# Moving the weight sums and a low part among the instructions of a feed-forward chunk, and four low parts of the head to adding transfers

## The chip, the cores and the metric

The kernel runs on one core of a Trainium2 chip. The metric is the device time of one execution in microseconds. A core has five engines that each work through their own instructions in order and wait for each other by semaphores: TensorE (PE in the profile; PEld is its loading of weights), VectorE (DVE), ScalarE (ACT), GpSimd (POOL) and SyncE (SP). SyncE starts the plain transfers here; GpSimd starts a few transfers that add what they bring to what stands at their destination.

## The reference

Two request groups of 512 and 256 tokens (768 in all, width 1024) go through two layers with shared weights: windowed attention in the first, a gated short convolution in the second. Each is followed by a feed-forward block of width 4096 and a gated input embedding. All is in float32. The change lies in the feed-forward block of both layers:

```python
h = rms_norm(x, norm_mlp[i])
x = x + jnp.square(jax.nn.relu(h @ mlp_w_up[i])) @ mlp_w_down[i]
gate = jax.nn.sigmoid(rms_norm(x, norm_ple[i]) @ ple_w_gate[i])
x = x + (p[i] @ ple_w_proj[i]) * gate
```

## The kernel before

**Precision.** TensorE multiplies a rounded format (float32r). To keep float32's accuracy each operand is split into a high part (ScalarE copies it, rounded) and a low part (VectorE subtracts the high part from the original). A product is then three matmuls: high by high, high by low, low by high. For a sum `s` the weights' parts are named `zhi`/`zlo` (s2 and s3), `whi`/`wlo` (the others) and `vhi`/`vlo` (w22).

**Seven products for eight.** Most blocks are multiplied by Strassen's scheme in Winograd's form: weights and activations are quartered, sums and differences of quarters are formed (weights: s1 to s4; activations: t1 to t4), and seven products replace eight. `product7` is one of them: 12 matmuls of 384 columns, in a fixed order of w11, s3, s2, w12, s1, w22, s4. The sums of weights are made by VectorE (`sums32`: L411 and L412; `sums14`: L416 and L417), their high part by ScalarE (L436), their low part by VectorE (L455). The four banks of results a, b, c, d are made by adding and by copying: `c` is a copy of a behind w11, `d` one behind s2, both by ScalarE, and `p` a copy of b to SBUF; the next product then writes on into a.

**Feed-forward.** It has 16 up chunks (u = 0 to 15, each makes 256 of the 4096 hidden features) and down chunks of the same size; after u=0 and u=1 follow, seven times, an up chunk with even u, two down chunks, and an up chunk with odd u. So from u=3 on two up chunks stand together, odd and even, and two down chunks behind them. Each job prepares the weights of the next (`v`, made by `make`), while its own come as `w`. Up chunks are `up_begun`/`up_first` (u=0), `up_plain` (u=1, without the seven products) and `up` (from u=2 on, where `first` is true for u=2 alone).

**What sets the order.** The order of instructions of TensorE, VectorE and ScalarE is the one in which the code is written (`manual_schedule`). In `up`, `late()` takes the next of eight steps that turn the activations of the chunk before into parts: the last square, two high parts, the sums, two more high parts (L356), and the two low parts of the sums (`low`, L362, VectorE). Between the products stand: the weights' sums and parts for the next chunk; the addition of a and p behind s1 (L1279), which must be done before product s4 writes on into a; the rectifications (L1031, VectorE), and the squares (L1034, ScalarE). The low part of s32 of the weights is made at the start of the next job by `w.low("s32")`, where `due` says that it is still missing. The next job's first copy (`c` at L1256, or the two `C` at L1307 of a down chunk) stands on ScalarE behind the two squares.

**The head.** `up_first` is the chunk u=0 of layer 0. Beside its plain products it makes the sums of activations of the input for m = 1, 2 and 3 (`Sums`: `t13`, `t42` on VectorE, `high` on ScalarE, `low` on VectorE), from two copies `q` (L327). Their parts are first read by the product s3 of u=2. `Weights7.added` (L442) already makes a low part without VectorE: ScalarE writes the negative of the high part, and a transfer by GpSimd adds the original from outside of the chip.

Of the kernel before, what the change touches and what calls it, by code (L numbers as in the profile page):

```python
# [11 lines left out]
F32 = mybir.dt.float32  # L12
F32R = mybir.dt.float32r
AF = mybir.ActivationFunctionType
ALU = mybir.AluOpType
# [32 lines left out]
def trunk_kernel(ctx: ExitStack, tc: tile.TileContext, a: dict, out: bass.AP):  # L48
    nc = tc.nc
    act, dve, pe = nc.scalar, nc.vector, nc.tensor  # L50
# [54 lines left out]
    def bank(tag, name):  # L105
        return psum.tile([P, 512], F32, tag=tag, name=name, bufs=BANKS[tag])
# [45 lines left out]
    def big(name, dt=F32):  # L152

        nonlocal turn
        if more is None:
            return tmp.tile([P, T], dt, tag="t", name=name)
        turn += 1
        return tmp.tile([P, T], dt, tag=f"q{turn % 6}", name=name, bufs=1)
# [174 lines left out]
    class Sums:  # L333
# [26 lines left out]
        def low(self, i):  # L360
            hi, lo = self.t[i]
            dve.tensor_tensor(lo[:], (self.q1, self.q2)[i][:], hi[:].bitcast(F32), ALU.subtract)  # L362

        def steps(self):
            return [
                self.t13,
                lambda: self.high(0),
                self.t42,
                lambda: self.high(1),
                lambda: self.low(0),  # L370
                lambda: self.low(1),
            ]
# [24 lines left out]
    class Weights7:  # L397
# [44 lines left out]
        def added(self, group):  # L442

            self.high(group)
            self.due.remove(group)
            hi, lo, _ = self.parts[group]
            act.activation(lo[:], hi[:].bitcast(F32), AF.Copy, scale=-1.0)
            nc.gpsimd.dma_start(lo[:], self.src[group == "second"], accum_op=ALU.add)
# [20 lines left out]
    def product7(ps, w, key, xs, start, step=P, col=0):  # L469

        hi, lo = w.w[key]
        rhs = xs[QS7[key]]
        ks = [(slice(step * i + col, step * i + col + P), rhs[i]) for i in range(512 // step)]
        terms = [(hi[:, c], p) for c, ps_ in ks for p in ps_] + [(lo[:, c], ps_[0]) for c, ps_ in ks]
        for i, (a, b) in enumerate(terms):
            pe.matmul(ps, lhsT=a, rhs=b, start=start and i == 0, stop=i == len(terms) - 1, skip_group_check=True)  # L476
# [544 lines left out]
    def mlp(l, norm, nxt, w, places, early, product=None, begun=None):  # L1021
# [8 lines left out]
        def rectified(t, src, o, e, op):  # L1030
            dve.scalar_tensor_tensor(t[:, o:e], src, 0.0, r[:, o:e], op, ALU.mult)  # L1031

        def squared(t):
            act.activation(t[:], t[:], AF.Square)  # L1034

        def acts_of(u, y1, y2, rest):

            own = places[7 * (u % 2) : 7 * (u % 2) + 7]
            e = Acts(y1, y2, own, groups[u // 2], u % 2)
            if u < 2 * NG - 2:  # L1040
                return [
                    lambda: squared(rest),
                    lambda: e.highx(0),
                    lambda: (e.highx(1), e.lowx(0), e.lowx(1), e.t13()),
                    e.t42,
                    lambda: e.high(0),
                    lambda: e.high(1),
                    lambda: e.low(0),
                    lambda: e.low(1),
                ]  # L1050

            def whole(i, q):
                hi, lo = slot(own[2 * i], "act"), slot(own[2 * i + 1], "act")
                split(hi[:], lo[:], q[:])
                groups[u // 2].setdefault("whole", {})[u % 2, i] = hi[:], lo[:]

            return [lambda: squared(rest), lambda: whole(1, y2), lambda: whole(0, y1)]

        def late(n=1):

            for _ in range(n):
                if pend:
                    pend.pop(0)()

        def plain_block(ps, i, w, ks=range(KB)):
            for k in ks:
                m, h = PAIRED[k] % (KB // 2), PAIRED[k] // (KB // 2)
                c = slice(P * m, P * m + P)
                hi, lo = w.w[f"w{i + 1}{h + 1}"]
                for j, (wt, part) in enumerate(((hi, 0), (hi, 1), (lo, 0))):  # L1070
                    for o in range(2):
                        pe.matmul(
                            ps[o],
                            lhsT=wt[:, c],
                            rhs=xs[f"x{h + 1}{1 + o}"][m][part],
                            start=k == 0 and j == 0,
                            stop=k == KB - 1 and j == 2,
                        )
# [28 lines left out]
        def up_first(ps, w, v, parts, s1):  # L1107


            nonlocal r  # L1110
            plain_block(ps[0], 0, w, range(4))
            ss = norm.sum_squares(psum, parts=parts, tag="C")
            plain_block(ps[0], 0, w, range(4, KB))
            plain_block(ps[1], 1, w)
            logs, newton, result = norm.rstd_steps(psum, ss)
            logs()
            s1.t13()
            s1.t42()
            s1.high(0)
            s1.high(1)  # L1120
            newton()
            s2 = norm.copied(2, 6)
            result()
            r = norm.r
            v.added("second")
            s1.low(0)
            s1.low(1)
            v.high("direct")
            s2.t13()
            s2.high(0)  # L1130
            v.low("direct")
            s2.t42()
            s2.high(1)
            s3 = norm.copied(3, 7)
            s2.low(0)
            s2.low(1)
            y = [big(f"y{i + 1}") for i in range(2)]
            for i in range(2):
                for o in range(2):
                    rectified(y[i], ps[i][o], H * o, H * o + H, ALU.max)  # L1140
                if i == 0:
                    s3.t13()
                    s3.high(0)
                    squared(y[0])
                    s3.t42()
                    s3.high(1)
                    s3.low(0)
                    s3.low(1)
            pend.extend(acts_of(0, *y, y[1]))
            return v  # L1150

# [89 lines left out]
        def up(u, w, make, then):  # L1241


            first = u == PLAIN[l]
            w.low("s32")
            w.split("s14")
            if not first:
                late()
            v = make()
            seven = isinstance(v, Weights7)  # L1250
            a = bank("A", "a")[:, :H]
            product7(a, w, "w11", xs, True)
            if not first:
                late()
            c = bank("A" if first else "C", "c")[:, :H]
            act.activation(c, a, AF.Copy)  # L1256
            late(5 if first else 1)
            w.split("w22")
            late()
            b = bank("A" if first else "B", "b")[:, :H]  # L1260
            product7(b, w, "s3", xs, True)
            p = big("p")[:, :H]
            act.activation(p, b, AF.Copy)
            if seven:
                v.sums32()
            product7(a, w, "s2", xs, False)
            d = bank("B", "d")[:, :H]
            act.activation(d, a, AF.Copy)
            late(2)
            if seven:  # L1270
                v.sums14()
                v.high("s32")
            late()
            product7(c, w, "w12", xs, False)
            if seven:
                v.high("direct")
            product7(a, w, "s1", xs, False)
            y1, y2 = big("y1"), big("y2")
            dve.tensor_tensor(y2[:, H:], a, p, ALU.add)  # L1279
            rectified(y1, c, 0, H, ALU.max)  # L1280
            late()
            if seven:
                v.low("direct")
            else:
                v = [then(0)]
            product7(d, w, "w22", xs, False)
            dve.tensor_tensor(y2[:, :H], d, p, ALU.add)
            rectified(y2, y2[:], 0, T, ALU.min)
            squared(y2)
            product7(a, w, "s4", xs, False)  # L1290
            rectified(y1, a, H, T, ALU.max)
            pend.extend(acts_of(u, y1, y2, y1))
            return v
# [80 lines left out]
        with tc.manual_schedule(engines={ET.Activation, ET.PE, ET.DVE}):  # L1374
            for i, (job, *args) in enumerate(jobs):

                def make():

                    if i + 1 == len(jobs):
                        return None  # L1380
                    what, *n = jobs[i + 1]
                    if what is not down:
                        return up_chunk(l, *n)
                    k = (KB // 2) * n[0] + 2 * n[1]
                    return Weights7(a_down[k], a_down[k + 1])
# [544 lines left out]
```

## Time and profile before

| | |
|---|---|
| median of three runs | 1682.73 us (1681.79 to 1683.66) |
| the profiled execution | 1684.2 us |
| span of its records | 1682.2 us |
| TensorE's granted clock over the span | 0.996 |
| instructions in the span | 24112 |

A row of the timeline gives the start and the duration in microseconds, the engine, the line, the operation, what it writes and reads, and how many instructions were merged into the row; in brackets, how long the engine had been idle before it and for whom it waited. TensorE's matmuls overlap, so a row's end is later than the next row's start. A row of the waits gives who waited for whom, then the total in microseconds, the number of times and the longest.

### The profile page before, as it was taken

Reading aid. Unit: us, or ns where it says so; the run is one execution under the profiler, and the core shown is the slowest. Engines: PE = TensorE matmul, PEld = TensorE weight load, DVE = VectorE, ACT = ScalarE, POOL = GpSimd, SP = SyncE. Lnnn points to the kernel's source line nnn. Section 1 sums busy time; section 2 is a strip of 40 time slices with the busy share of each in tenths; the row PEclk is TensorE's granted clock in tenths of the full one; section 3 lists DMA queues with packets and bytes.
Section 4 is the critical chain, followed back from the end, with each engine's and each line's share of the span. In section 5 each row is a group of like instructions: output and inputs, shape, how many; then the busy total and the mean of one; then the engine's idle time right before and its main releaser. Section 6 shows DMA issues by size and latency. Waiting matters only on the chain.

```text
span 1682.2 us, 24112 instructions
## 1 busy us (share of the span) xinstructions
PE 1645.5 (98%) x9410; PEld 1586.8 (94%) x9410; DVE 1411.9 (84%) x2302; ACT 905.8 (54%) x1451; POOL 20.3 (1%) x46
## 2 busy tenths in 40 slices
PE   8999999999999999999999999999999999999996
PEld 6888788999999999999999999999999999999985
DVE  6598888899999999977788787768999898998776
ACT  6377756755555455545654334545555545554544
POOL 0211000000000000000000000000000000000000
PEclk9999999999999999999999999999999999999998
DMA  8755322411221222231312222121222122122222
GB/s 262 192 152 143 92 66 74 121 63 63 76 76 64 75 76 66 73 104 63 101 60 76 76 75 76 61 66 54 73 75 76 63 76 76 63 76 88 82 76 95
DMA packets 47107, 145.64 MB, mean 87 GB/s; under 512 B 6112, under 2 KB 9184, under 8 KB 46992
## 3 DMA queue, kind: packets, MB, share of 16 engines
q1 hardware_dynamic: 45168, 139.89, 26.1%
q0 software_dynamic: 1824, 4.20, 1.2%
q8 instruction: 74, 1.21, 0.3%
q14 instruction: 41, 0.34, 0.1%
HBM read 124.14 MB, written 10.48 MB: 80 GB/s over the span
## 4 chain that ended last, share of the span: by engine, by line
PE 58%; DVE 30%; ACT 7%; issue 3%; DMA 1%; SPq 0%; DVEq 0%; ACTq 0%
PE a L476 17%; PE mm L129 9%; PE mm L138 8%; PE b L476 4%; PE B L476 4%; PE C L476 3%; DVE t L362 3%; DVE wlo L455 3%; DVE y L1031 3%; PE gate L138 3%; DVE zlo L455 2%; DVE act L395 1%; PE pt L743 1%; DVE sum L412 1%; ACT y L1034 1%
## 5 line engine op out<-in xcount | busy, mean ns | idle before, releaser
L436 ACT ACTIVATE whi<-sum 128x1024 fp32r<-128x1024 f32 x67 | 70.5, 1053 | 150.7 <-PE a L476 146.8
L1034 ACT ACTIVATE y<-y 128x768 f32<-128x768 f32 x64 | 53.7, 840 | 135.5 <-DVE y L1031 135.5
L476 PE MATMUL a<-xs,whi 128*128 128x384 f32 x624 | 121.9, 337 | 2.4 <-DVE y L1279 1.7
L476 PEld LDWEIGHTS a<-xs,whi 128*128 128x128 f32 x624 | 110.0, 188 | 3.1 <-DVE y L1279 2.0
L476 PE MATMUL a<-t,zhi 128*128 128x384 f32 x536 | 109.1, 337 | 0.0
L476 PE MATMUL a<-t,whi 128*128 128x384 f32 x536 | 108.8, 336 | 0.0
L476 PE MATMUL b<-t,zhi 128*128 128x384 f32 x536 | 108.8, 336 | 0.0
L476 PE MATMUL a<-act,whi 128*128 128x384 f32 x448 | 96.5, 337 | 0.0
L476 PEld LDWEIGHTS a<-t,whi 128*128 128x128 f32 x536 | 94.9, 188 | 0.0
L476 PEld LDWEIGHTS a<-t,zhi 128*128 128x128 f32 x536 | 94.6, 188 | 0.2 <-ACT c L1752 0.2
L476 PEld LDWEIGHTS b<-t,zhi 128*128 128x128 f32 x536 | 94.8, 188 | 0.0
L455 DVE TENSOR_TENSOR wlo<-wraw,whi 128x1024 fp32r<-128x1024 f32 x70 | 85.3, 1218 | 7.6 <-ACT whi L436 7.6
L455 DVE TENSOR_TENSOR wlo<-sum,whi 128x1024 fp32r<-128x1024 f32 x67 | 81.9, 1222 | 8.9 <-ACT whi L436 8.9
L1312 DVE TENSOR_TENSOR x<-x,a 128x384 f32<-128x384 f32 x112 | 60.7, 552 | 33.8 <-PE a L476 33.5
L436 ACT ACTIVATE zhi<-sum 128x1024 fp32r<-128x1024 f32 x67 | 71.0, 1060 | 23.0 <-DVE sum L412 23.0
L138 PE MATMUL mm<-xs_mix,whi 128*128 128x512 f32 (+1 forms) x320 | 83.0, 342 | 0.0
L455 DVE TENSOR_TENSOR zlo<-sum,zhi 128x1024 fp32r<-128x1024 f32 x67 | 81.5, 1217 | 0.0
L476 PEld LDWEIGHTS a<-act,whi 128*128 128x128 f32 x448 | 79.8, 188 | 0.0
L436 ACT ACTIVATE whi<-wraw 128x1024 fp32r<-128x1024 f32 x72 | 75.7, 1051 | 6.2 <-PE C L476 6.2
L356 ACT ACTIVATE t<-y 128x768 fp32r<-128x768 f32 x56 | 47.1, 842 | 40.6 <-DVE y L347 29.9
L476 PE MATMUL a<-xs,wlo 128*128 128x384 f32 x312 | 67.1, 336 | 0.0
L455 DVE TENSOR_TENSOR vlo<-wraw,vhi 128x512 fp32r<-128x512 f32 x67 | 46.1, 689 | 24.8 <-ACT vhi L436 24.8
(338 smaller groups left out, 4503.7 us busy)
## 6 DMA issues: line engine op xcount, KB each, us to landing
wraw<-in_up SPq DMA_DIRECT2D x64, 512.0 KB, 3.5
wraw<-in_down SPq DMA_DIRECT2D x64, 512.0 KB, 3.5
wraw<-in_w_in SPq DMA_DIRECT2D x24, 512.0 KB, 3.5
wraw<-in_gate SPq DMA_DIRECT2D x16, 512.0 KB, 3.4
pj<-pjs SPq DMA_DIRECT2D x16, 384.0 KB, 3.8
wraw<-in_w_q SPq DMA_DIRECT2D x8, 512.0 KB, 4.5
wraw<-in_w_out SPq DMA_DIRECT2D x8, 512.0 KB, 3.4
x_in<-in_x SPq DMA_DIRECT2D x8, 384.0 KB, 7.3
```

The source lines that it names most:

```text
L129: pe.matmul(t, lhsT=w, rhs=x[:, o:e], start=first and i == 0 and j == 0, stop=last and i == n - 1 and j == 2)
L138: pe.matmul(ps[:, o:e], lhsT=w, rhs=x[:, o:e], start=i == 0 and j == 0, stop=i == n - 1 and j == 2,)
L356: act.activation(t[0][:], (self.q1, self.q2)[i][:], AF.Copy)
L362: dve.tensor_tensor(lo[:], (self.q1, self.q2)[i][:], hi[:].bitcast(F32), ALU.subtract)
L395: dve.tensor_tensor(lo[:], self.q2[:], hi[:].bitcast(F32), ALU.subtract)
L412: dve.tensor_tensor(a[:, 512:], a[:, :512], r2[:, 512:], ALU.add)
L436: act.activation(hi[:], src, AF.Copy)
L455: dve.tensor_tensor(lo[:], src, hi[:].bitcast(F32), ALU.subtract)
L476: pe.matmul(ps, lhsT=a, rhs=b, start=start and i == 0, stop=i == len(terms) - 1, skip_group_check=True)
L1031: dve.scalar_tensor_tensor(t[:, o:e], src, 0.0, r[:, o:e], op, ALU.mult)
L1034: act.activation(t[:], t[:], AF.Square)
L1312: dve.tensor_tensor(t[:, o : o + H], t[:, o : o + H], f, op)
```

## The change

The diff, whole:

```diff
@@ class Sums
         def low(self, i):
             hi, lo = self.t[i]
             dve.tensor_tensor(lo[:], (self.q1, self.q2)[i][:], hi[:].bitcast(F32), ALU.subtract)
+
+        def added(self, i):
+
+            hi, lo = self.t[i]
+            act.activation(lo[:], hi[:].bitcast(F32), AF.Copy, scale=-1.0)
+            nc.gpsimd.dma_start(lo[:], (self.q1, self.q2)[i][:], accum_op=ALU.add)
@@ up_first
             s2.t13()
             s2.high(0)
             v.low("direct")
+            s2.added(0)
             s2.t42()
             s2.high(1)
             s3 = norm.copied(3, 7)
-            s2.low(0)
-            s2.low(1)
+            s2.added(1)
             y = [big(f"y{i + 1}") for i in range(2)]
...
                     s3.t42()
                     s3.high(1)
-                    s3.low(0)
-                    s3.low(1)
+                    s3.added(0)
+                    s3.added(1)
@@ up
             late(2)
             if seven:
-                v.sums14()
                 v.high("s32")
-            late()
+            if not first:
+                late()
             product7(c, w, "w12", xs, False)
...
             dve.tensor_tensor(y2[:, H:], a, p, ALU.add)
             rectified(y1, c, 0, H, ALU.max)
+            if first:
+                late()
+            if seven:
+                v.sums14()
             late()
             if seven:
                 v.low("direct")
...
             product7(a, w, "s4", xs, False)
+            if seven:
+                v.low("s32")
             rectified(y1, a, H, T, ALU.max)
```

Three things are done. In every up chunk from u=2 on whose next job has sums, `sums14` goes from ahead of product w12 to behind the addition of a and p and the first rectification. The low part of s32 goes ahead of the chunk's last rectification; the call at the start of the next job then finds nothing due. In u=2 one `late()` goes behind the addition as well. In the head, the four subtractions of the sums m = 2 and 3 become four ScalarE instructions and four transfers by GpSimd that add `q` to what ScalarE wrote. TensorE's and SyncE's instructions stay in their order.

On VectorE, an odd chunk of layer 0 (u=3) behind the sums of s32, before: L416 and L417 are `sums14`, L362 the second low part of the activations' sums (the row ahead of these is the first), L1279 the addition, L1031 rectifications, L455 low parts.

```order
L416 TENSOR_TENSOR sum<-wraw 128x512
L417 TENSOR_TENSOR sum<-wraw,sum 128x512
L362 TENSOR_TENSOR t_4536<-y_4156,t_4535 128x768
L1279 TENSOR_TENSOR y_4573<-a,p 128x384
L1031 SCALAR_TENSOR_TENSOR y_4572<-c,rstd_mlp_3851 128x384
L455 TENSOR_TENSOR wlo<-wraw,whi 128x1024
L1287 TENSOR_TENSOR y_4573<-d,p 128x384
L1031 SCALAR_TENSOR_TENSOR y_4573<-y_4573,rstd_mlp_3851 128x768
L1031 SCALAR_TENSOR_TENSOR y_4572<-a,rstd_mlp_3851 128x384
L455 TENSOR_TENSOR zlo<-sum,zhi 128x1024
```

The same place now (line numbers are larger by 6 to 12, L1285 is the addition):

```order
L362 TENSOR_TENSOR t_4540<-y_4157,t_4539 128x768
L1285 TENSOR_TENSOR y_4575<-a,p 128x384
L1037 SCALAR_TENSOR_TENSOR y_4574<-c,rstd_mlp_3851 128x384
L422 TENSOR_TENSOR sum<-wraw 128x512
L423 TENSOR_TENSOR sum<-wraw,sum 128x512
L461 TENSOR_TENSOR wlo<-wraw,whi 128x1024
L1297 TENSOR_TENSOR y_4575<-d,p 128x384
L1037 SCALAR_TENSOR_TENSOR y_4575<-y_4575,rstd_mlp_3851 128x768
L461 TENSOR_TENSOR zlo<-sum,zhi 128x1024
L1037 SCALAR_TENSOR_TENSOR y_4574<-a,rstd_mlp_3851 128x384
```

The two sums stand behind the addition and the rectification of c, and `zlo` has passed the rectification of a.

On VectorE, the chunk u=2 of layer 0 from the end of the sums of s32 on, now; before, L416 and L417 and the first L362 stood ahead of the addition:

```order
L418 TENSOR_TENSOR sum<-sum,wraw 128x512
L1285 TENSOR_TENSOR y_4157<-a,p 128x384
L1037 SCALAR_TENSOR_TENSOR y_4156<-c,rstd_mlp_3851 128x384
L362 TENSOR_TENSOR t_4121<-y_3986,t_4120 128x768
L422 TENSOR_TENSOR sum<-wraw 128x512
L423 TENSOR_TENSOR sum<-wraw,sum 128x512
L362 TENSOR_TENSOR t_4124<-y_3987,t_4123 128x768
```

Here the addition follows the sums of s32 directly.

On ScalarE, the head (end of u=0 of layer 0) now: L356 writes a high part, the new L367 the negative of a high part into the place of the low part, L327 copies q, L1040 squares:

```order
L356 ACTIVATE t_3865<-q 128x768
L367 ACTIVATE t_3866<-t_3865 128x768
L356 ACTIVATE t_3873<-q 128x768
L327 ACTIVATE q<-x,vec 128x768 x2
L367 ACTIVATE t_3874<-t_3873 128x768
L356 ACTIVATE t_3888<-q 128x768
L1040 ACTIVATE y_3882<-y_3882 128x768
L356 ACTIVATE t_3894<-q 128x768
L367 ACTIVATE t_3889<-t_3888 128x768
L367 ACTIVATE t_3895<-t_3894 128x768
L1040 ACTIVATE y_3883<-y_3883 128x768
```

The four rows of L367 are new there, and the four rows of L362 that stood on VectorE in the head are gone.

## The prediction

> **What bounds the kernel now.** I read the page first, then who waited for whom on TensorE, then the timeline of the chunks that the change touches.
>
> ```profile
> PE 1645.5 (98%) x9410; PEld 1586.8 (94%) x9410; DVE 1411.9 (84%) x2302; ACT 905.8 (54%) x1451; POOL 20.3 (1%) x46
> ```
> ```profile
> PE b L476 <- DVE zlo L455: 1.8, 8, 0.4
> ...
> PE a L476 <- DVE y L1279: 1.7, 1, 1.7
> ```
>
> TensorE is busy for 98% of the span, so only its remaining gaps can be won, and any new gap is paid in full. Of its listed waits, two kinds lie in the code that changes. Once, it waits 1.7 us for the addition of a and p (L1279). Eight times it waits for `zlo`, the low part of the sums s2 and s3, at the first product that uses it, b. More such stops are too short to be listed as waits; the timeline shows them. One pair of up chunks and the down chunk behind it, in layer 0:
>
> ```profile
> 391.63 1.57 PE L476 MATMUL a<-xs,whi 128*128 128x384 f32 x8
> 391.83 0.55 DVE L1312 TENSOR_TENSOR x<-x,a 128x384 f32<-128x384 f32 x1 [0.51 <-PE a L476]
> ...
> 400.96 0.69 DVE L416 TENSOR_TENSOR sum<-wraw 128x512 f32<-128x512 f32 x1
> ...
> 402.12 1.57 PE L476 MATMUL d<-t,vhi 128*128 128x384 f32 x8
> 402.16 0.95 DVE L362 TENSOR_TENSOR t<-y,t 128x768 fp32r<-128x768 f32 x1
> 403.03 0.55 DVE L1279 TENSOR_TENSOR y<-a,p 128x384 f32<-128x384 f32 x1
> ...
> 406.73 0.85 ACT L1034 ACTIVATE y<-y 128x768 f32<-128x768 f32 x1 [4.46 <-DVE y L1031]
> 407.02 1.22 DVE L455 TENSOR_TENSOR zlo<-sum,zhi 128x1024 fp32r<-128x1024 f32 x1
> 408.44 0.83 ACT L1034 ACTIVATE y<-y 128x768 f32<-128x768 f32 x1
> 409.72 0.47 ACT L1256 ACTIVATE c<-a 128x384 f32<-128x384 f32 x1
> 410.52 1.56 PE L476 MATMUL a<-t,zhi 128*128 128x384 f32 x8
> ...
> 410.99 0.96 DVE L395 TENSOR_TENSOR act<-y,act 128x768 fp32r<-128x768 f32 x1 [0.58 <-ACT act L386]
> ...
> 422.85 1.22 DVE L455 TENSOR_TENSOR zlo<-sum,zhi 128x1024 fp32r<-128x1024 f32 x1
> 423.13 0.86 PE L476 MATMUL b<-t,zhi 128*128 128x384 f32 x4
> 424.12 0.62 PE L476 MATMUL b<-t,zlo 128*128 128x384 f32 x2
> 424.94 0.85 ACT L1307 ACTIVATE C<-a 128x384 f32<-128x384 f32 x2
> 425.62 0.68 PE L476 MATMUL a<-t,zhi 128*128 128x384 f32 x3
> ```
>
> How to read it. Twelve matmuls of a product take 2.09 us (chunk u=3's d starts at 402.12; eight of them are listed with 1.57, the last one drawn to its end), so four take 0.70. At the down chunk b starts at 423.13 and its low part should start at 423.83; it starts at 424.12, just behind the end of `zlo` at 422.85 + 1.22 = 424.07. That is **0.29 us lost**, and about 0.10 more to get going again (below). VectorE is the reason: from 410.99, where it last waited for ScalarE, to 424.07 the timeline shows no gap in it. Three further things will be needed. Two neighbours on VectorE start closer than the duration listed: 0.87 apart for the 0.95 of L362, so 0.08 less. A result of TensorE is there 0.20 after the next product began: L1312 had waited for a and starts at 391.83, the next a at 391.63. And ScalarE stands in order: square of y2 (406.73), high part of s1 and s4, square of y1 (408.44), a first step of the activations, then the copy c (409.72), which ends at 410.19. The product at 410.52 writes on into a, the bank that c copies, and so may not start before that copy has ended. The same holds for C at 424.94 and the a at 425.62. Its slack is 0.33 in the one and 425.62 − (424.94 + 0.47) = **0.21 us** in the other. I call these copies the edge.
>
> **The change, part by part.**
>
> *Sums s1 and s4 behind the addition (odd chunk u=3).* No instruction is added. Before, from 400.96 on, VectorE ran L416 and L417, the second low part (402.16) and L1279 (403.03). Now the second low part takes the place at 400.96 and VectorE is free at 401.83, but product s1, which the addition reads, is there only at 402.12 + 0.20 = 402.32. So VectorE **stands for 0.49 us** in which it worked before; the addition comes 0.71 earlier, but TensorE wants it only for s4 and didn't wait for it here. All the work that followed still stands ahead of the rectification of y2, which thus comes 0.49 later, and with it ScalarE's square: 406.73 becomes 407.22.
>
> *Low part ahead of the last rectification.* `zlo` passes the rectification of y1, an instruction of 384 columns like L1279, worth 0.55 − 0.08 = 0.47 of VectorE: with the 0.49 lost it starts at 407.04 instead of 407.02, so nothing is won. The rectification of y1 starts 1.14 behind it, at 408.18, ends at 408.73 and its square could start some 0.1 behind that, at 408.82. ScalarE itself is ready for that at 408.44 + 0.49 = 408.93, so this half costs nothing, by a margin of 0.11. What is late next is the copy c: 409.72 + 0.49 = 410.21, ended at 410.68, and TensorE gets a at about 410.73, not 410.52: 0.21, and 0.10 for the restart.
>
> *The even chunk u=4.* VectorE is fed by those ScalarE steps, so it runs 0.49 later from 410.99 on, without a gap; the addition is now later than its product and waits for nothing. `zlo` gives 0.47 back: 422.85 becomes 422.87, ending at 424.09. TensorE, 0.31 late, wants the low part at 424.14 and no longer waits. But C is copied at 424.94 + 0.49 = 425.43 and its first half ends at 425.90, so a starts at 425.95 instead of 425.62, and a restart adds 0.10: **+0.43 us for the pair**, where the old wait is replaced by one on ScalarE. In layer 1:
>
> ```profile
> 1157.57 0.68 DVE L416 TENSOR_TENSOR sum<-wraw 128x512 f32<-128x512 f32 x1
> ...
> 1158.40 1.57 PE L476 MATMUL d<-t,vhi 128*128 128x384 f32 x8
> ...
> 1166.59 0.84 ACT L1307 ACTIVATE C<-a 128x384 f32<-128x384 f32 x2
> ...
> 1167.28 0.86 PE L476 MATMUL a<-t,zhi 128*128 128x384 f32 x4
> ...
> 1201.75 0.68 DVE L416 TENSOR_TENSOR sum<-wraw 128x512 f32<-128x512 f32 x1
> ...
> 1202.88 1.57 PE L476 MATMUL d<-t,vhi 128*128 128x384 f32 x8
> ...
> 1225.73 0.85 ACT L1307 ACTIVATE C<-a 128x384 f32<-128x384 f32 x2
> ...
> 1226.43 0.86 PE L476 MATMUL a<-t,zhi 128*128 128x384 f32 x4
> ```
>
> The pair: free at 1201.75 + 0.87 = 1202.62, product there at 1203.08, idle 0.46; C ends at 1225.73 + 0.46 + 0.47 = 1226.66, a at 1226.71 + 0.10 against 1226.43: **+0.38**. Each layer has six such pairs (u=3 and 4, up to 13 and 14): 6 × 0.43 + 6 × 0.38 = **+4.9 us**.
>
> *Chunk u=2 of layer 1.* Here the first low part too goes behind the addition. VectorE is free at 1157.57, the product is there at 1158.60: 1.03 idle, and no work between it and the square is saved. C ends at 1166.59 + 1.03 + 0.47 = 1168.09, a starts at 1168.14 + 0.10 against 1167.28: **+1.0 us**.
>
> *Head and chunk u=2 of layer 0.*
>
> ```profile
> 330.26 1.75 ACT L327 ACTIVATE q<-x,vec 128x768 f32<-128x768 f32 x2
> ...
> 334.93 0.83 ACT L356 ACTIVATE t<-q 128x768 fp32r<-128x768 f32 x1
> ...
> 337.72 0.85 ACT L1034 ACTIVATE y<-y 128x768 f32<-128x768 f32 x1 [1.96 <-DVE y L1031]
> ...
> 347.04 1.56 PE L476 MATMUL b<-t,zhi 128*128 128x384 f32 x8
> ...
> 355.42 1.57 PE L476 MATMUL d<-t,vhi 128*128 128x384 f32 x8
> ...
> 358.77 0.55 DVE L1279 TENSOR_TENSOR y<-a,p 128x384 f32<-128x384 f32 x1
> ...
> 359.37 1.66 PE L476 MATMUL a<-xs,whi 128*128 128x384 f32 x8 [1.68 <-DVE y L1279]
> ...
> 365.71 0.85 ACT L1307 ACTIVATE C<-a 128x384 f32<-128x384 f32 x2
> 366.40 0.86 PE L476 MATMUL a<-t,zhi 128*128 128x384 f32 x4
> ```
>
> Four subtractions of 0.95 leave VectorE; four negations of about 0.84 go to ScalarE, four adding transfers to the GpSimd queue. Before, ScalarE sat 1.96 ahead of the square at 337.72 for a rectification queued behind two of the four. Now it runs two negations behind the high part at 334.93: 334.93 + 3 × 0.75 = 337.18, a gain of 0.54. If the high part itself comes sooner (its sums then wait only for the copies of q, done at 332.01, and three steps of 0.59 more) it is up to 1.2. I take 1.1; 0.54 is the low end. L1279 follows L412 directly, at about 356.70 − 1.1 = 355.6, when the product is just there (355.62), and TensorE's 1.68 goes. Late next is, again, C: its chain starts 1.08 earlier, so its first half ends at 365.71 − 1.08 + 0.47 = 365.10 and a starts at 365.15 + 0.10 against 366.40: **−1.15 us**, though the wait removed was larger. The restart price is seen here: eight matmuls behind the stop take 1.66 against 1.56.
>
> ```profile
> wlo<-in_up POOLq DMA_DIRECT2D x2, 512.0 KB, 6.6
> ```
> ```profile
> DMA to landing us min/median/max: 5.7/6.6/7.4
> ```
> ```profile
> 108.75 2.21 POOL L679 DMA_DIRECT2D bias<-skew  x4 [48.91 <-DVE sm L732]
> ```
>
> No row shows an adding transfer out of the chip's own memory; the nearest are two from outside of 512 KB, 5.7 to 7.4 us. The new ones have 384 KB. The last two are issued from about 337 on; side by side they land by 345.3. Their first reader is the product b at 347.04 (third and fourth block, so some 0.8 later). I take nothing for them. The low end is nothing too, the high end is the fourth rival.
>
> *Sum.* −1.15 + 2.6 + 2.3 + 1.0 = **+4.7 us**. The profiled execution took 1684.2 (span 1682.2 and 2.0 around it) and would take 1688.9; the three plain runs have their median at 1682.73, 1.5 below it, and I carry the difference over: **1687.4 us**.
>
> **The rivals.**
>
> *Wash.* The stand for s1 is partly made up, since 0.1 or 0.2 more overlap at the edge is all it takes: its slack was 0.21 to 0.33. With 0.1 instead of 0.4 for a pair, 12 × 0.1 + 1.0 − 1.15 = +1.0: 1683.8. For it: the margins are tenths. Against it: ScalarE's steps from the square to C stand behind each other without a gap.
>
> *Faster.* If the result of s1 were ready by 401.83 the addition wouldn't stand, `zlo` would come 0.47 sooner and its waits would go: the 0.39 of a pair twelve times and once at u=2 of layer 1, with 1.15 at the head: −6.2, so **1676.5**. It decides at an idle of 0.16: up to there C's slack of 0.21, less 0.05 to hand over, holds. Against it is the row at 402.12, to which the order before L1279 is tied.
>
> *Larger loss.* The three stops of a pair don't overlap, or the 0.11 in front of y1's square is gone: 0.21 + 0.10 + 0.42 and three restarts, less 0.39, is 0.64 a pair. 12 × 0.64 + 1.0 − 0.5 = +8.2: 1690.9.
>
> *Late transfers.* If the last two run one behind the other at 7.4 each, the second lands at 337.4 + 14.8 = 352.2 and is wanted in the second product, at 347.04 + 2.09 + 1.2 = 350.3: 1.9 more, 1689.3. Against it: four transfers of that queue were issued within 2.21 us (108.75), less than the 5 to 7 that each needs. The Trainium skill, page SBUF — State Buffer, section "SBUF: two separate sides", says that GpSimd cannot write the descriptors of such a transfer while VectorE holds the port they share; by that rule each could start one VectorE instruction later, an estimate of 1.2 us each, and this rival would cost 4 rather than 2. The two adding transfers of before were issued among VectorE work and landed in 7.4 at most, which doesn't bear it out.
>
> **How the numbers follow.** Forecast with its spread (1686.2 to 1690) 55 in 100, larger loss 8, late transfers 4, wash 22, faster 11. A measurement of this kernel tells about 0.2%, or 3.4 us, from no change. Slower by more than that: 0.67; within it: 0.22; faster: 0.11. The range goes from the low side of the wash to the larger loss, **1681.5 to 1691**; it leaves out the faster case and some tail above.
>
> **What would show it.** VectorE idle ahead of the addition, put down to PE a, some 0.5 in odd chunks and 1.0 at layer 1's u=2. TensorE's waits at b for `zlo` gone or 0.1, and new ones at a for ScalarE's c and C. At u=2 of layer 0 no wait for the addition. No wait of TensorE for the t of the head. It is wrong if the edge copies keep their times, or if t is waited for.

## The result and the profile after

The changed kernel is **slower**: a median of 1690.8 us (1688.73 to 1692.83, 6 runs) against 1683.2 us (1681.11 to 1685.54, 6 runs) of the kernel before. The ratio is 1.005, with a 95% interval of 1.004 to 1.006, so about 7 to 10 us. The forecast was +4.7 us (1687.4) with 1691 as its upper end: the direction was right, the size too small. The profiled execution took 1692.5 us (span 1690.5) against 1684.2 (span 1682.2).

The waits of TensorE in the changed kernel:

```profile
PE a L482 <- DMA t<-q: 1.6, 1, 1.6
...
PE a L482 <- DVE wlo L461: 0.7, 2, 0.4
PE b L482 <- DVE zlo L461: 0.5, 2, 0.2
```

The wait for the addition is gone and that for `zlo` shrank from eight listed times to two. A wait for the adding transfers of the head (t<-q) is new. Stops that are too short for this list show in the waits of the weight loading (PEld), which counts from the end of the load before, so its sums are larger than what TensorE loses. First before, then after:

```profile
PEld b L476 <- DVE zlo L455: 8.3, 17, 0.7
```
```profile
PEld a L482 <- ACT C L1319: 6.4, 14, 0.5
PEld b L482 <- DVE zlo L461: 5.1, 17, 0.6
PEld a L482 <- ACT c L1262: 4.7, 12, 0.4
```

The stops at ScalarE's copies are new: at c (L1262) once in each of the twelve pairs, at C (L1319) in each pair and in both chunks u=2. The stops at `zlo` became shorter, but not fewer. VectorE's own waits, before and after:

```profile
DVE y L1279 <- PE a L476: 10.7, 2, 5.4
```
```profile
DVE y L1285 <- PE a L482: 18.6, 16, 5.4
```

VectorE now stands for product s1 at fourteen more additions. The pair of up chunks shown in the prediction, after (this execution ran 0.99 later at that place):

```profile
403.31 0.56 DVE L1285 TENSOR_TENSOR y<-a,p 128x384 f32<-128x384 f32 x1 [0.41 <-PE a L482]
...
408.22 0.85 ACT L1040 ACTIVATE y<-y 128x768 f32<-128x768 f32 x1 [4.95 <-DVE y L1037]
...
410.82 0.85 PE L482 MATMUL b<-t,zlo 128*128 128x384 f32 x4
...
411.22 0.47 ACT L1262 ACTIVATE c<-a 128x384 f32<-128x384 f32 x1
...
411.74 1.66 PE L482 MATMUL a<-t,zhi 128*128 128x384 f32 x8
...
423.94 1.22 DVE L461 TENSOR_TENSOR zlo<-sum,zhi 128x1024 fp32r<-128x1024 f32 x1
...
424.45 0.86 PE L482 MATMUL b<-t,zhi 128*128 128x384 f32 x4
...
425.22 0.62 PE L482 MATMUL b<-t,zlo 128*128 128x384 f32 x2
...
426.36 0.51 PE L482 MATMUL b<-t,zlo 128*128 128x384 f32 x2
426.49 0.84 ACT L1319 ACTIVATE C<-a 128x384 f32<-128x384 f32 x2
427.02 0.64 PEld L482 LDWEIGHTS a<-t,zhi 128*128 128x128 f32 x4 [0.46 <-ACT C L1319]
427.02 0.96 PE L482 MATMUL a<-t,zhi 128*128 128x384 f32 x4
```

VectorE is idle for 0.41 ahead of the addition (0.49 was worked out; the row counts from the listed end of its neighbour, 0.08 later than the working does). ScalarE's square follows later, the copy c ends at 411.69, and a starts at 411.74, where 410.82 + 0.70 = 411.52 was its turn: 0.22 lost. Two matmuls take 0.35, so behind 426.36 the next a was due at 426.71; the first copy C ends at 426.96, and a starts at 427.02: 0.31 lost. Both stops are those that the prediction named. At b, whose low part was due at 425.15 and starts at 425.22, 0.07 and a restart of 0.10 are left.

In the head, the four issues of the new transfers on GpSimd:

```profile
326.88 0.91 POOL L454 DMA_DIRECT2D wlo<-in_up  x1 [19.19 <-ACT wlo L453]
...
332.80 0.88 POOL L368 DMA_DIRECT2D t<-q  x1 [5.00 <-DVE q L347]
...
337.17 0.90 POOL L368 DMA_DIRECT2D t<-q  x1 [3.50 <-ACT t L367]
...
341.42 0.88 POOL L368 DMA_DIRECT2D t<-q  x1 [3.35 <-DVE y L347]
...
345.69 0.90 POOL L368 DMA_DIRECT2D t<-q  x1 [3.40 <-ACT y L1040]
```
```profile
352.31 0.44 PE L482 MATMUL a<-t,zhi 128*128 128x384 f32 x1 [1.60 <-DMA t<-q]
```

The four of L368 start some 4.3 us apart, though the negation that the first waits for had ended at 328.97 (L367, 328.12 + 0.85) and the last two at about 336.6; the engines named in the brackets had long been done. Each is issued about 0.3 us after the one before it has landed; the first three land 4.1, 3.9 and 4.0 us after their issue. The last takes 6.6, to 352.29, and TensorE, in the second product of u=2 that reads the sums (s2), stands for 1.60 us. This last one had company: a plain transfer of 512 KB (wraw<-in_down, by SyncE) was issued at 346.1. Landed within 4.1 us it would have been there at 349.79, ahead of its reader's turn at 350.54 (seven matmuls of 0.174 behind 349.32). So the stop needs both, the late issue and the slow last landing; that the plain transfer slowed it was not tried.

Where the time went: how much later the product s2 (the first a behind b) starts than before, at some places of the program.

| place | before, us | after, us | later by |
|---|---|---|---|
| u=2, layer 0 | 349.12 | 349.32 | 0.20 |
| second down chunk behind it | 381.10 | 382.09 | 0.99 |
| down chunk behind u=3 and 4 | 425.62 | 427.02 | 1.40 |
| second down chunk behind these | 440.28 | 441.79 | 1.51 |
| second down chunk behind the sixth pair | 736.37 | 740.30 | 3.93 |
| u=2, layer 1 | 1152.13 | 1156.01 | 3.88 |
| second down chunk behind it | 1181.93 | 1186.88 | 4.95 |
| second down chunk behind the sixth pair | 1536.84 | 1544.66 | 7.82 |

Twelve pairs cost 2.94 + 2.87 = 5.8 us, u=2 of layer 1 costs 1.07, and u=2 of layer 0, where 1.15 was to be won, costs 0.79. Together that is 7.7 us, 2.9 more than forecast, of which 1.94 lie at u=2 of layer 0 and 0.9 in the pairs.

### The profile page after: what moved, and what is told of

The parts are those of the page before. It is cut to its first block, busy times and chain, and to the rows that moved or that the text cites. A ratio compares the mean times of both kernels' runs of the same rounds, so it can differ in the third digit from the quotient of the medians.

```text
span 1690.5 us, 24128 instructions
## 1 busy us (share of the span) xinstructions
PE 1654.3 (98%) x9410; PEld 1587.6 (94%) x9410; DVE 1410.1 (83%) x2298; ACT 909.4 (54%) x1455; POOL 23.8 (1%) x50
## 4 chain that ended last, share of the span: by engine, by line
PE 67%; DVE 21%; ACT 9%; issue 2%; DMA 1%; SPq 0%; DVEq 0%; ACTq 0%
PE a L482 22%; PE mm L129 9%; PE mm L138 8%; PE b L482 4%; PE gate L138 4%; PE B L482 3%; PE C L482 3%; PE c L482 3%; ACT y L1040 3%; DVE wlo L461 2%; DVE y L1037 2%; DVE t L362 2%; ACT whi L442 2%; PE pt L749 1%; PE d L482 1%
## 5 line engine op out<-in xcount | busy, mean ns | idle before, releaser
L1040 ACT ACTIVATE y<-y 128x768 f32<-128x768 f32 x64 | 53.7, 840 | 143.7 <-DVE y L1037 143.7
L356 ACT ACTIVATE t<-y 128x768 fp32r<-128x768 f32 x56 | 47.1, 844 | 39.3 <-DVE y L347 28.0
```

Of the source, the lines that this page charges most:

```text
L356: act.activation(t[0][:], (self.q1, self.q2)[i][:], AF.Copy)
```

## The experiments

Theory A: the pairs lose because VectorE stands at the addition, and ScalarE's copies c and C, which TensorE waits for, come that much later; the head loses because the adding transfers are issued one at a time. Its rivals: the transfers are slow by themselves (B) or disturb more than their one wait (C); the rectification of y1 behind `zlo` delays the squares, not the sums (D). Each run has its kernel before on the same chip; ratios are to that.

**More room for the descriptors of GpSimd's transfers.** A parameter of the program, which the kernel sets to 512, to 2048.

```diff
-BACC = dict(dynamic_dma_scratch_size=512)
+BACC = dict(dynamic_dma_scratch_size=2048)
```

> The changed kernel with four times the room for the descriptors of GpSimd's transfers (2048 for 512). Theory A: in the changed kernel each adding transfer is issued only when the one before has landed (issues at 332.80, 337.17, 341.42 and 345.69, landing 3.9 to 6.6 later), because the room holds one; with more room they are issued as soon as ScalarE's negations are ready, about 329, 333, 336 and 337, TensorE's wait of 1.6 us for t at u=2 of layer 0 goes, and the time falls by about 1.9 us against the changed kernel (still some 6.4 above before). Theory B: the transfers are slow by themselves, or are held up by VectorE: the spacing of about 4.3 us and the wait of 1.6 stay, and the time stays.

Measured: 1687.08 us against 1682.17, ratio 1.0028 (1.0016 to 1.0040). The issues:

```profile
326.83 0.86 POOL L368 DMA_DIRECT2D t<-q  x1 [1.67 <-DVE q L351]
...
330.98 0.87 POOL L368 DMA_DIRECT2D t<-q  x1 [3.29 <-DVE q L351]
...
333.75 1.79 POOL L368 DMA_DIRECT2D t<-q  x2 [1.89 <-ACT t L367]
```
```profile
DMA to landing us min/median/max: 4.5/5.5/7.7
```

The last two are now issued behind each other, all are out 11 us earlier than before this edit (this execution runs some 2 us ahead), and no wait for t is left. In flight together they take a little longer, 4.5 to 7.7 us against 3.9 to 6.6. B falls. From u=2 of layer 0 (2.24 ahead of the kernel before) to the second down chunk behind it (3.34 ahead) this kernel wins 1.10 us, where 1.15 was predicted and the changed kernel loses 0.79. The whole comes to +4.9 us by the medians, less than the expected 6.4, which the interval (+2.7 to +6.7) just holds; by the places of the table above the kernel loses 5.8 us from u=2 of layer 0 on.

**The head back on VectorE**, the chunks changed.

```diff
-            s2.added(0)
...
-            s2.added(1)
+            s2.low(0)
+            s2.low(1)
...
-                    s3.added(0)
-                    s3.added(1)
+                    s3.low(0)
+                    s3.low(1)
```

> The changed kernel with the four low parts of the head back on VectorE; the feed-forward chunks stay changed. Theory A (the loss of some 0.5 us for each of twelve pairs of up chunks comes from the order on VectorE): the pairs keep it, u=2 of layer 1 keeps its 1.0, so +6 to +7.5 us against before; the wait for t goes, but at u=2 of layer 0 VectorE is late again, so about the same time as the changed kernel or 1 less. Theory C (the transfers disturb more than their one wait): most of the loss goes, +2 us or less.

Measured: 1688.97 us, ratio 1.0040 (1.0025 to 1.0055), +6.7. The pairs keep their loss (6.0 us for the twelve, by the places of the table). At u=2 of layer 0 another wait stands in the place of the one for t:

```profile
361.24 0.62 PE L482 MATMUL a<-act,wlo 128*128 128x384 f32 x2 [1.33 <-DVE wlo L461]
```

The low part for w11 of the down chunk is late, since VectorE is as late as before and TensorE, which no longer stops for the addition, meets it in the next job's first product. C falls.

**The head alone**, chunks as before (the head's part of the diff only).

> The kernel before with the four adding transfers of the head alone. Theory A: the pairs are as before, stops of 0.4 at b for zlo stay; at u=2 of layer 0 the addition comes about 1.1 earlier, its wait of 1.68 shrinks or goes, but TensorE waits for t instead, 1.6 or more: the sum is between -1 and +0.5 us. Theory C: slower by over 2 us.

Measured: 1680.56 us, ratio 0.9993 (0.9983 to 1.0002): no difference, or 1 us faster. TensorE's waits:

```profile
PE a L482 <- DMA t<-q: 1.6, 1, 1.6
PE b L482 <- DVE zlo L461: 1.4, 7, 0.2
```

The wait for the addition (1.7) is replaced by one for the transfers (1.6). Between u=2 and the second down chunk it wins 0.69 us, and the pairs cost nothing (0.03 us for the twelve).

**The sums alone.**

```diff
             if seven:
-                v.sums14()
                 v.high("s32")
-            late()
+            if not first:
+                late()
...
             rectified(y1, c, 0, H, ALU.max)
+            if first:
+                late()
+            if seven:
+                v.sums14()
             late()
```

> The kernel before with the sums s1 and s4 behind the addition alone (and the first chunk's step with them); the low part of s32 stays behind the last rectification. Theory A (VectorE stands 0.5 at the addition, and ScalarE's copies c and C come that much later): c late by 0.2 to 0.3 in even chunks, zlo 0.5 later than before, so the stop at b grows from 0.4 to about 0.55 to 0.6, together +0.5 a pair, +6 to +7.5 us in all. Theory D (the rectification of y1 behind zlo delays the squares, not the sums): no new wait at c, and within 1.5 us of before.

Measured: 1689.33 us, ratio 1.0043 (1.0029 to 1.0057), +7.2. The stop at a for c and the stop at b, which is longer than before:

```profile
407.60 1.34 PEld L476 LDWEIGHTS a<-t,zhi 128*128 128x128 f32 x8 [0.38 <-ACT c L1256]
407.60 1.66 PE L476 MATMUL a<-t,zhi 128*128 128x384 f32 x8
...
420.31 0.86 PE L476 MATMUL b<-t,zhi 128*128 128x384 f32 x4
...
421.54 0.62 PE L476 MATMUL b<-t,zlo 128*128 128x384 f32 x2 [0.37 <-DVE zlo L455]
```

The b's low part was due at 421.01 and started at 421.54, 0.53 late (0.29 before). The twelve pairs cost 6.8 us by the places of the table, more than in the changed kernel (5.8). So the sums carry the loss of the pairs by themselves, through c and through `zlo`; a wait for C, which theory A named too, is not in the list of this run. D falls.

**The low part alone.**

```diff
             product7(a, w, "s4", xs, False)
+            if seven:
+                v.low("s32")
             rectified(y1, a, H, T, ALU.max)
```

> The kernel before with the low part of s32 ahead of the last rectification alone; the sums stay ahead of the addition. Theory A: zlo comes 0.47 earlier, the stops at b for zlo go (0.4 a pair); the squares keep their times, since ScalarE isn't ready for y1 any sooner; but TensorE now reaches a 0.4 earlier than before and meets the copy C, which ends where it did: about 0.24 and a restart of 0.1 are given back. So 0 to -0.1 a pair, -1.5 to +0.5 us in all, with new waits of TensorE at a behind C. Theory D (the rectification behind zlo delays squares and copies): +0.3 to 0.5 a pair, +4 to +6 us.

Measured: 1680.46 us against 1682.11, ratio 0.9989 (0.9980 to 0.9998). The waits at b are gone from the list; a now stops at C:

```profile
421.65 0.51 PE L476 MATMUL b<-t,zlo 128*128 128x384 f32 x2
421.71 0.85 ACT L1309 ACTIVATE C<-a 128x384 f32<-128x384 f32 x2
422.24 0.65 PEld L476 LDWEIGHTS a<-t,zhi 128*128 128x128 f32 x4 [0.40 <-ACT C L1309]
422.24 0.96 PE L476 MATMUL a<-t,zhi 128*128 128x384 f32 x4
```

Due at 422.00, a starts at 422.24, when the first copy has ended (421.71 + 0.47): 0.24 lost, as expected. By the places of the table the twelve pairs won 0.06 each. The median's gain of 1.65 is a little more than the expected 1.5, within the interval.

**The low part, and the square of y1 behind the copies C.**

```diff
@@ down
             w.split("s14")
-            if h == 0:
-                late()
             v = make()
             a = [bank("A", "a")[:, :H] for _ in range(2)]
             products(a, "w11", True)
             c = copies("C", a)
+            if h == 0:
+                late()
```

> As the run before (zlo ahead of the last rectification, sums where they were), and in the first down chunk the square of y1 behind the two copies C on ScalarE instead of ahead of them. Theory A: C ends some 0.75 earlier, the stop at a doesn't come, and the whole 0.4 of each of the thirteen stops is won: -4 to -6 us against before. Rival (ScalarE is late anyway, the square then delays the high parts and p behind it): -1 us or less.

Measured: 1676.51 us, ratio 0.9969 (0.9958 to 0.9980), −5.2 us (−5.6 by the medians). The same place:

```profile
423.65 0.84 ACT L1309 ACTIVATE C<-a 128x384 f32<-128x384 f32 x2
...
424.33 0.51 PE L476 MATMUL b<-t,zlo 128*128 128x384 f32 x2
424.43 0.83 ACT L1034 ACTIVATE y<-y 128x768 f32<-128x768 f32 x1
...
424.68 0.86 PE L476 MATMUL a<-t,zhi 128*128 128x384 f32 x4
```

The copies start before b ends, the square comes behind them, and a follows b after 0.35 us, without a stop. The rival falls. The copy behind the square was what held the earlier `zlo` back.

**The changed kernel with the same move.**

> The changed kernel, with the square of y1 behind the copies C in the first down chunk. Theory A: of the stops of a pair (c 0.2, b 0.1, C 0.3 and restarts) the last goes, so a pair costs about what it did before; left are the wait for t (1.8), 0.5 to 1.0 at u=2 of layer 1, and what VectorE's head gains: 0 to +4 us against before, some 5 less than the changed kernel. Rival (the loss lies at the stop at c and moves on): +6 us or more.

Measured: 1683.54 us, ratio 1.0010 (1.0001 to 1.0019), +1.7. A pair costs some 0.1 more than before instead of 0.5. What is left is the stop at c, which the sums cause, and the head:

```profile
352.29 0.44 PE L482 MATMUL a<-t,zhi 128*128 128x384 f32 x1 [1.71 <-DMA t<-q]
...
411.35 1.66 PE L482 MATMUL a<-t,zhi 128*128 128x384 f32 x8
```

**What the runs point to**: the kernel before, with the adding transfers of the head and room of 2048, the earlier low part, and the square behind C. The sums stay ahead of the addition.

> What the runs point to, together: the kernel before, with the four adding transfers of the head and 2048 of room for descriptors, the low part of s32 ahead of the last rectification, and the square of y1 behind the copies C in the first down chunk; the sums s1 and s4 stay ahead of the addition. Theory A: -4 to -6 us from the stops at b, -1 to -3 from the head (no wait for t, the wait for the addition at u=2 shrinks): -5 to -8 us against before. Rival (gains at the head are taken back by the next stop, at b of the first down chunk): -4 to -5 us.

Measured: **1674.62 us** (1673.74 to 1676.15, 5 runs) against 1682.11, ratio 0.9955 (0.9942 to 0.9969): −7.6 us, faster than both kernels.

```profile
PE a L482 <- DVE y L1285: 0.3, 1, 0.3
```

No wait for t and none for `zlo` in the list; of the wait for the addition 0.3 is left. From u=2 to the second down chunk of layer 0 it wins 1.81 us.

## Why the prediction was right and wrong

*The bound.* Right: what the change won or lost shows as stops of TensorE, tenths of a microsecond in the chunks and 1.60 us in the head. Those that were expected in the chunks are found where they were named.

*VectorE at the addition.* Right. It stands 0.41 in the pair shown, fourteen times more than before in all, and the run with the sums alone loses as much as the whole change. The stop at c (0.22 for 0.21 worked out) and the one at C (0.31) are as described; at b 0.07 and a restart are left, where the working left nothing; C sets the time behind it.

*The size of a pair.* Too small: 0.49 measured in layer 0 and 0.48 in layer 1 (5.8 us for twelve) for 0.43 and 0.38. The step that failed is "the addition is now later than its product and waits for nothing" in even chunks. TensorE, stopped at c, delivers s1 later as well; the addition of u=4 starts at 418.34, 0.20 behind the d at 418.14, thus when its product is just there:

```profile
418.14 1.57 PE L482 MATMUL d<-t,vhi 128*128 128x384 f32 x8
418.34 0.56 DVE L1285 TENSOR_TENSOR y<-a,p 128x384 f32<-128x384 f32 x1
```

With the 0.99 taken off, that is 417.35 for the 417.28 that the working gives (low part at 416.41, and 0.87), and the copy C starts at 425.50 for the 425.43 of the working: both 0.07 later. The restart of 0.10 comes on top of the start of a, as worked out.

*The low part ahead of the last rectification.* Nearly right: while C stands behind the square it gives little (0.06 us a pair alone, and 5.8 instead of 6.8 us for the twelve beside the sums), and it doesn't cost either. What the prediction didn't see is how cheaply the obstacle can be moved.

*u=2 of layer 1.* Right: 1.07 for 1.0, though by two more stops than were named, 0.5 for the low part of the down chunk's first weights and 0.4 for `zlo`. The last in the row, C, sets the sum.

*The head.* Here the prediction failed, in the step "I take nothing for them". −1.15 was the term, +0.79 came, and the wait for t, which was to show the prediction wrong, is there. The transfers were taken to fly side by side, by a row of four issued within 2.21 us. But those are plain transfers of 96 KB to 32 partitions (GpSimd starts 32 such too, not adding ones alone), and further rows of the same queue of the kernel before show it being held once some are out:

```profile
46.11 3.40 POOL L679 DMA_DIRECT2D bias<-skew  x6 [44.81 <-DMA skew<-brow]
50.22 1.19 POOL L679 DMA_DIRECT2D bias<-skew  x2 [0.71 <-issue]
51.58 0.53 POOL L679 DMA_DIRECT2D bias<-skew  x1 [0.18 <-issue]
52.91 1.22 POOL L679 DMA_DIRECT2D bias<-skew  x2 [0.79 <-issue]
```

Six go out without a gap; the seventh starts at 50.22, 0.3 behind the landing of the first (46.11 + 3.8 = 49.91), and GpSimd idles there between transfers that wait for no engine. So four within 2.21 us said nothing of the limit. In the run with 2048 of room ten go out without a gap at the same place:

```profile
44.88 5.48 POOL L685 DMA_DIRECT2D bias<-skew  x10 [43.57 <-DMA skew<-brow]
```

The rival on late transfers had the mechanism, one behind the other, and nearly the price: 1.9, where the first eight matmuls of s2 take 3.27 (352.59 − 349.32) instead of 1.40, so 1.87. But it was given 4 in 100. With room the term came out as 1.10 won. That the kernel with room then lies at +4.9 us by the medians, so near the +4.7 forecast, is partly luck: its pairs still cost 6.0 for 4.9. The rest of that part was right in its outcome: the wait for the addition is gone, and C sets the end. With room VectorE even reaches the addition 1.4 us earlier (1.1 was taken) and stands 0.31 for its product.

*The rivals.* "Larger loss" came near the measured time (1690.9 for 1690.8) by luck: it has 0.64 for a pair, where 0.48 was measured, and 0.5 won at the head, where 0.79 was lost. "Faster" fell with the idle of 0.41, above the 0.16 from which it decides. The rule of the Trainium skill (page SBUF — State Buffer, section "SBUF: two separate sides") on the port that VectorE and GpSimd share isn't needed for what was seen: with room, each transfer is issued 0.3 to 0.5 us after the end of its negation, among the same VectorE work.

## What to carry to other kernels

Work that stands ahead of an instruction which must wait for another engine anyway isn't in the way: it fills the wait. Moving it behind that instruction uncovers the wait, and the delay runs on through every engine fed by it, up to the one that sets the time. An earlier part is worth only what the next edge allows, so look for the copy or square that stands behind it in another engine's order, and move that too. Before work is given to GpSimd's queue, look for idle between its transfers that no engine explains, and count how many of that size can be out at once.

## What the runs showed of the hardware

- With 512 of room for descriptors, a transfer of 128 rows by GpSimd is issued only when the one before has landed (4.3 us apart); with 2048, two were issued within 1.79 us and three were out at once. Of transfers of 96 KB to 32 partitions, six go out behind one another with 512 and ten with 2048. How the limit follows from the room was not tried.
- An adding transfer of 384 KB from the chip's own memory to itself lands 3.9 to 4.1 us after its issue when it is the only one out, 6.6 beside a plain transfer of 512 KB, and 4.5 to 7.7 when several of GpSimd's are out.
- A stop of TensorE costs some 0.10 us more than the wait: eight matmuls behind it take 1.66 us for 1.56.
